# First norm with a weight spread by products, meta queries two blocks earlier, output projections in a held order

## The chip, the cores and the metric

The kernel runs on one core of a Trainium2 chip. A core has a matrix engine (TensorE, PE in the profile; its weight loads are a row of their own, PEld), VectorE (DVE), ScalarE (ACT), GpSimd (POOL) and SyncE (SP), which here issues every DMA. The metric is the device time of one execution, in microseconds; less is better. Where the time goes is read from one execution that the hardware profiler recorded.

## The reference

Two layers of a hybrid decoder, on 1024 tokens of 1024 columns with 16 learned meta tokens ahead of them (1040 rows), all in fp32:

```
h = rms_norm(x, norm_g)                       # row factor times weight
z = h @ w_in                                  # 1024 x 6408: aq ak av ag | mq mk mv mi mf mo mgate
ya = window_attention(rope(norm(q)), rope(norm(k)), v, sink) * silu(ag)   # 16 heads, 2 kv heads
hm = mlstm(silu(conv(mq, mk)), mv, mi, mf)    # 4 heads, chunkwise, with a carried state
ym = rms_norm(hm) * sigmoid(mo) * silu(mgate)
x  = x + concat(ya, ym) @ w_out               # 2048 x 1024
```

The window is 128 keys; the meta tokens are visible to every query and are themselves queries in the first layer. The meta rows are dropped at the end, so the second layer does not compute their attention or output (`first_q` is 1 there).

## The kernel before, in words

Rows are cut into nine tiles (`TT`): tile 0 has the 16 meta rows, tiles 1 to 8 have 128 rows each. For the gates and the loads of activations the same rows are cut into three chunks of columns (`CH`: 272, 384, 384). Every fp32 product is made of three products in the fast fp32r format: both operands are split into a high and a low part, and high x high, high x low and low x high are accumulated in PSUM (`mm3`, L178). For the short tile 0, the three parts are stacked as 48 rows (`HM`), so that two products do.

**Weights.** A weight piece is loaded by SP into one of two raw buffers, copied to its high part by ACT and subtracted to its low part by POOL or DVE (`wpair`, L147, for w_in; `wout`, L168, for w_out). Eight pairs of high and low parts stand in a ring (`RING`). In `wout` DVE takes each third piece and POOL the other two.

**A layer** goes through these stages: keys and values (`kv_tasks`, L452), the first queries, eight pairs of heads j = 0 to 7 with gate and query projections woven in, the mLSTM heads with their projections woven in, and the output projection (from L1091), which at the end of layer 0 also norms the rows for layer 1.

**First norm** (layer 0, `first_norm`, L312). For each row tile ACT squares and sums both halves (L318), POOL multiplies the halves by the norm weight `G` (L320), which a DMA has spread over 128 partitions (L456), and POOL raises the mean square to -1/2 (L279). DVE multiplies by that factor (L282), PE transposes (L288), ACT and DVE split the result into `H` (L291, L292). Tile 0 comes first, and two tiles are normed ahead of the one that is projected (`projN`, L200).

**Attention.** Block b of a pair of heads runs in four steps that lie two and three blocks apart: s1 the scores and the softmax (L618), s2 the transposes of the probabilities (L657), s3 and s4 the products with the values (L682, L695). s3 and s4 share one PSUM bank, `O`. The queries of the meta tokens for the next pair are transposed in s3 of block 5 into free columns of that bank (`q_meta_turn`, L688), and split into the query stack behind s4 (`q_put`, L559 to L564: two ACT copies, two DVE subtractions). The next pair's block 0 reads them in s1 (L628).

**Output projection.** The 16 column blocks of the mixer's result lie in DRAM (`spool`), the last two in SBUF. All are loaded and split (L1096 to L1109). Then come four groups: tiles 0 to 4 for the left and the right 512 columns, then tiles 5 to 8 likewise. In a group each weight piece is multiplied with each tile of the group (`product`, L1123 to L1135), and one PSUM bank per tile collects the sum; banks are dealt from three pools in turn. At the end of a group, for each tile: load the residual `xr` (L1154), add (L1157), store, and in layer 0 square for the next norm, in place in the bank (L1162). In the second half of columns, the norm of the tile follows (`norm_tile`, L274). In the last group the last eight pieces are held back, and each tile is finished alone.

**What sets the order.** The program is traced once; a planner then runs it in a simulated timeline and fixes the order of each engine's instructions by readiness and by the order in which they were traced. Semaphores enforce the dependencies; each engine then works its list strictly in order. `pin` (L68) makes PE's instructions keep the traced order among themselves while `in_order[0]` is set: in the first queries and the attention, but before the change not in the first norm, the mLSTM and the output projections. `tc.high_priority` lifts instructions in the planner's heap. Tile pools (16 units of 1152 columns, five of 384 (`t`), four of 512 (`p512`), two raw buffers) make an instruction wait until a buffer is free.

## Time and profile before

| | |
|---|---|
| median of 3 runs | 1997.38 us (1996.06 to 1997.59) |
| profiled execution | 1995.97 us, its span 1994.2 us |
| PE busy | 1916.2 us, 96% of the span |
| DVE, ACT, POOL busy | 55%, 53%, 47% |
| mean granted PE clock | 0.990 |
| DMA | 147.71 MB, mean 74 GB/s |

How to read it: a row of the timeline has start, duration, engine, line and operation, output and inputs, and in brackets how long the engine was idle before and what released it. A row of the waits has who waited for what, the total in microseconds, how often, and the longest. A row of a window has its stretch and length, then for PE, PEld, DVE, ACT and POOL the busy time with the number of instructions, then the granted PE clock, the DMA engines' share and GB/s. A row of a group has line, operation, shapes and count, then busy time and mean nanoseconds, then the idle time before. Matmuls are pipelined, so that a busy PE row need not be PE at its peak; idle time in it, though, is real.

### The profile page before, as it was taken

How to read it: one execution, taken by the hardware profiler on the slowest of the kernel's cores; microseconds unless marked ns; L12 is line 12 of the kernel's file. 1: busy time of each engine (PE TensorE's matmuls, PEld its weight loads, DVE VectorE, ACT ScalarE, POOL GpSimd, SP SyncE). 2: the span in 40 equal slices, each digit the busy share in tenths (PEclk: the TensorE clock that was granted, in tenths of full speed). 3: DMA queues.
4: the chain of work that ended last, by engine and by line, in shares of the span. 5: the costliest groups of instructions: out<-in, count | busy, mean ns of one | idle time of the engine just before them, and what ended most of it. 6: DMA issues, size and time to landing. Idle time of an engine off the chain costs nothing. (4 is left out here: it accounts for less than half of the span.)

```text
span 1994.2 us, 36168 instructions
## 1 busy us (share of the span) xinstructions
PE 1916.2 (96%) x12823; PEld 1806.1 (91%) x12823; DVE 1099.9 (55%) x2969; ACT 1062.6 (53%) x3133; POOL 929.9 (47%) x1116
## 2 busy tenths in 40 slices
PE   6999899999999999989999999999999999999899
PEld 6899899999999999867879999999999999997787
DVE  8767767666445364541435677776573636347111
ACT  5567767655454544642324678777364545446221
POOL 7544544335555454553335345444365453646331
PEclk9999999999999999999999999999999999999999
DMA  5111111111212122453541111112122221217443
GB/s 160 43 33 42 42 44 37 35 53 45 57 47 69 36 59 58 146 170 115 162 144 49 48 36 51 45 36 58 38 58 62 39 76 38 61 47 232 145 141 106
DMA packets 149796, 147.71 MB, mean 74 GB/s; under 512 B 14952, under 2 KB 122768, under 8 KB 149616
## 3 DMA queue, kind: packets, MB, share of 16 engines
q1 hardware_dynamic: 149616, 145.41, 25.1%
q8 instruction: 101, 1.65, 0.4%
q14 instruction: 79, 0.65, 0.1%
HBM read 122.01 MB, written 23.29 MB: 73 GB/s over the span
## 5 line engine op out<-in xcount | busy, mean ns | idle before, releaser
L183 PE MATMUL pj<-H,RING 128*128 128x384 f32 (+2 forms) x3456 | 578.4, 323 | 0.3 <-ACT t L838 0.3
L183 PEld LDWEIGHTS pj<-H,RING 128*128 128x128 f32 x3456 | 546.1, 189 | 2.9 <-issue 0.7
L160 POOL TENSOR_TENSOR RING<-raw,RING 128x512 fp32r<-128x512 f32 (+1 forms) x196 | 260.6, 1337 | 137.8 <-ACT RING L159 125.4
L222 PE MATMUL pj<-RING,H 128*128 128x256 f32 (+1 forms) x1920 | 270.0, 287 | 1.9 <-DVE w1k L190 1.9
L222 PEld LDWEIGHTS pj<-RING,H 128*128 128x128 f32 x1920 | 244.0, 190 | 2.3 <-DVE w1k L190 2.2
L222 PE MATMUL pj<-H,RING 128*128 128x384 f32 (+2 forms) x1152 | 217.7, 327 | 3.0 <-DVE u L564 3.0
L175 POOL TENSOR_TENSOR RING<-raw,RING 128x512 fp32r<-128x512 f32 x88 | 115.0, 1311 | 196.8 <-ACT RING L174 192.4
L183 PE MATMUL pj<-RING,H 128*128 128x256 f32 x1536 | 200.8, 285 | 2.6 <-DVE H L292 1.5
L183 PEld LDWEIGHTS pj<-RING,H 128*128 128x128 f32 x1536 | 189.0, 189 | 4.0 <-DVE H L292 1.7
L174 ACT ACTIVATE RING<-raw 128x512 fp32r<-128x512 f32 x128 | 80.7, 632 | 202.2 <-DMA raw<-in_w_out_dram 134.1
L222 PEld LDWEIGHTS pj<-H,RING 128*128 128x128 f32 x1152 | 180.7, 191 | 3.8 <-PE T L668 1.3
L159 ACT ACTIVATE RING<-raw 128x512 fp32r<-128x512 f32 (+1 forms) x196 | 122.9, 629 | 73.3 <-DMA raw<-in_w_in_dram 48.2
L713 POOL TENSOR_TENSOR u<-u,w1k 128x128 f32<-128x128 f32 (+1 forms) x136 | 63.4, 466 | 176.8 <-DVE w1k L709 169.4
L175 DVE TENSOR_TENSOR RING<-raw,RING 128x512 fp32r<-128x512 f32 x40 | 31.5, 788 | 194.0 <-ACT RING L174 194.0
L679 POOL TENSOR_SCALAR_AFFINE_SELECT p<-p 128x512 fp32r<-128x512 f32 x112 | 72.2, 645 | 133.7 <-DVE p L675 131.1
L649 ACT ACTIVATE t<-S,mx 128x145 f32<-128x145 f32 (+1 forms) x272 | 100.3, 373 | 62.6 <-DVE mx L646 54.5
L882 POOL TENSOR_TENSOR p<-u,p 128x258 fp32r<-128x258 f32 x64 | 46.7, 730 | 169.2 <-ACT p L881 169.1
L1135 PE MATMUL pj<-RING,H 128*128 128x512 f32 x352 | 112.9, 400 | 7.1 <-DVE p L1157 5.8
L1135 PE MATMUL pss<-RING,H 128*128 128x512 f32 x352 | 113.5, 402 | 1.3 <-ACT H L1104 1.3
L824 DVE SCALAR_TENSOR_TENSOR t<-u,cw,t 128x384 f32<-128x384 f32 (+1 forms) x144 | 109.1, 757 | 2.6
L628 PE MATMUL S<-u 128*128 128x272 f32 (+2 forms) x544 | 87.5, 280 | 19.3 <-DVE u L563 16.3
L654 ACT ACTIVATE t<-t,mx 128x144 f32<-128x144 f32 (+1 forms) x272 | 97.6, 406 | 13.6 <-DVE mx L651 13.1
(342 smaller groups left out, 3834.0 us busy)
## 6 DMA issues: line engine op xcount, KB each, us to landing
raw<-in_w_out_dram SPq DMA_DIRECT2D x128, 256.0 KB, 2.8
raw<-in_w_in_dram SPq DMA_DIRECT2D x100, 256.0 KB, 2.8
raw<-in_w_in_dram SPq DMA_DIRECT2D x192, 128.0 KB, 2.3
spool<-u SPq DMA_DIRECT2D x56, 192.0 KB, 1.9
p<-x SPq DMA_DIRECT2D x24, 256.0 KB, 4.4
t<-spool SPq DMA_DIRECT2D x28, 192.0 KB, 3.5
p<-spool SPq DMA_DIRECT2D x28, 192.0 KB, 3.6
u<-em SPq DMA_DIRECT2D x8, 576.0 KB, 6.9
```

Of the source, the lines that this page charges most:

```text
L159: sc.activation(hi, raw[:, :, 0:o], AF.Copy)
L160: eng.tensor_tensor(lo, raw[:, :, 0:o], hi, op=ALU.subtract)
L174: sc.activation(hi, raw, AF.Copy)
L175: (ve if i % 3 == 2 else gp).tensor_tensor(lo, raw, hi, op=ALU.subtract)
L183: pin(pe.matmul(out, a, b, start=(i == 0), stop=(i == n - 1)))
L222: pin(pe.matmul(out(), x, y, start=(k + i == 0), stop=(k == n - 1 and i == 2)))
L628: pin(pe.matmul(S[:p, h, o + 2 - 2 * h:o + 2 - 2 * h + kn], lq, Ks[i][:, k0:k0 + kn], start=(i == 0), stop=(i == 1)))
L649: sc.activation(P[:p, 145 * h:145 * h + 145], S[:p, h, 1 + 127 * h:146 + 127 * h], AF.Exp, bias=mx[:p, 0, h:h + 1], accum_out=mx[:p, 1, h: ...
L654: sc.activation(Pn, Pn, AF.Copy, scale=mx[:p, 2, h:h + 1])
L679: gp.affine_select(OW, HL, [[0, 4], [1, 128]], ALU.is_ge, 0.0, base=0, channel_multiplier=-1)
L824: ve.scalar_tensor_tensor(z, RAW[:, t0 + i:t0 + i + n], wcol(i), z, ALU.mult, ALU.add)
L1135: pin(pe.matmul(ps[:p, :], a, b, start=(i + n == 0), stop=(i == 15 and n == len(terms) - 1)))
```

## The change

**First norm.** The norm weight is loaded as one row, and two products with a row of ones spread it over 128 partitions into two PSUM banks. One DVE operation per half multiplies the rows by factor and weight at once, in place (`norm_pre`), instead of a POOL and a DVE operation; `norm_tile` is cut into `norm_pre` and `norm_half`. Tiles are taken in the order 1, 2, 0, 3 to 8; the loads of the first tile stand ahead of the constants, and the rope tables, masks and parameters come later. ACT's squares of a tile are placed behind the evacuation of an earlier tile (`tc.issue_after`), the rope tables behind the last power on POOL, and the conv parameters' transpose behind PE's last key and value product. The first queries' weights are asked for at the fourth tile.

**Meta queries.** The transpose for the next pair is placed in block 3 instead of block 5.

**Output projections.** Loading and splitting the activations is a function of column block and chunk (`y_split`): chunks 0 and 1 are interleaved with the weights of the first group, chunk 2 with those of the second. Banks rotate over six. Each group ends with a tail of three pieces (six in the last group), in which each tile is finished alone. The residual's load is placed behind the group's last weight load. Squares are written to another bank (`pt`). POOL splits all of a group's first nine pieces; from the tenth on DVE and POOL take turns. In layer 0 the norm of tiles 0 to 4 is taken from DRAM again and made in the third group, the one of tiles 5 to 8 in the last group, as half tiles between products (`turns`); three half tiles are carried into the keys and values of layer 1 (`carry`). From the second group on, PE keeps the traced order.

```diff
     cst = cp.tile([128, 166], F32, name="cst")
-    sy.dma_start(cst, I["cst"])
...
-        sy.dma_start(raw, I["w_out"][l][k * 128:(k + 1) * 128, c0:c0 + 512])
+        w_load[0] = sy.dma_start(raw, I["w_out"][l][k * 128:(k + 1) * 128, c0:c0 + 512]).ins
         hi, lo = [pair[:, a].rearrange("p a b -> p (a b)")[:, 0:512] for a in range(2)]
         sc.activation(hi, raw, AF.Copy)
-        (ve if i % 3 == 2 else gp).tensor_tensor(lo, raw, hi, op=ALU.subtract)
+        (ve if i > 8 and i % 2 else gp).tensor_tensor(lo, raw, hi, op=ALU.subtract)
...
-    def norm_tile(t, xh, ssq_ap, gbc):
...
+    def norm_pre(t, xq, ssq_ap, gbc):
...
-        gp.tensor_tensor(v[:p, 1:2], v[:p, 0:1], nhalf[:p, 0:1], op=ALU.pow)
-        for g in range(2):
-            if gbc is None:
-                ve.tensor_scalar(xh[g][:p, :], xh[g][:p, :], v[:p, 1:2], None, ALU.mult)
-            for i in range(2 if gbc is not None else 0):
-                xs = xh[g][:p, 256 * i:256 * i + 256]
-                ve.scalar_tensor_tensor(xs, xs, v[:p, 1:2], gbc[2 * g + i][:p, 0:256], ALU.mult, ALU.mult)
...
+        mark["POOL"] = gp.tensor_tensor(v[:p, 1:2], v[:p, 0:1], nhalf[:p, 0:1], op=ALU.pow).ins
+        for x, g in zip(xq, gbc):
+            ve.scalar_tensor_tensor(x[:p], x[:p], v[:p, 1:2], g[:p, 0:x.shape[1]], ALU.mult, ALU.mult)
+
+    def norm_half(t, g, xs):
+
+        t0, p = TT[t]
+        ps = bank("pt")
...
+            pin(pe.transpose(ps[:, k * p:(k + 1) * p], xs[k // n][:p, k % n * 128:k % n * 128 + 128], ident[:p, :p]))
+        src = ps[:, 0:4 * p].rearrange("p (k t) -> p k t", k=4)
+        hi = H[:, 4 * g:4 * g + 4, t0:t0 + p]
+        mark["ACT"] = sc.activation(hi, src, AF.Copy).ins
+        ve.tensor_tensor(H[:, 8 + 4 * g:12 + 4 * g, t0:t0 + p], src, hi, op=ALU.subtract)
...
     def first_norm(t, xt, G):
...
+        order = tc.issue_after(evac[-3]) if len(evac) > 2 else nullcontext()
...
-        xg = []
-        for i in range(2):
-            j = bank("pss") if i else bank("po")
-            sc.activation(j[:p, :], xt[:p, 512 * i:512 * i + 512], AF.Square, accum_out=st[:p, i:i + 1])
-            y = p512(F32)
-            gp.tensor_tensor(y[:p, :], xt[:p, 512 * i:512 * i + 512], G[:p, 512 * i:512 * i + 512], op=ALU.mult)
-            xg.append(y)
-        norm_tile(t, xg, st[:p, 0:2], None)
+        xh = [xt[:, 512 * i:512 * i + 512] for i in range(2)]
+        with order:
+            for i in range(2):
+                sc.activation(bank("po")[:p, :], xh[i][:p, :], AF.Square, accum_out=st[:p, i:i + 1])
+        norm_pre(t, xh, st[:p, 0:2], G)
+        norm_half(t, 0, xh[0:1])
+        evac.append(mark["ACT"])
+        norm_half(t, 1, xh[1:2])
...
         def kv_tasks():
+            ts = list(range(9))
+            kg = w1k()
+
+            def consts():
+                for i, (c, o) in enumerate(((0, 64), (0, 72), (1, 72), (1, 64))):
+                    gp.tensor_tensor(qrt[:, :, 8 * i:8 * i + 8], kcs[:, c], kg[:, o:o + 8]
+                                     .rearrange("p (a c) -> p a c", a=1).to_broadcast([128, 9, 8]), op=ALU.mult)
+                gp.tensor_scalar(qrt[:, :, 16:24], qrt[:, :, 16:24], -1.0, None, ALU.mult)
...
             if l == 0:
-                xt = {0: load_tile(0)}
-                G = unit()
-                sy.dma_start(G[:, 0:D], I["norm_g"][0].partition_broadcast(128))
-                xt[1], xt[2] = load_tile(1), load_tile(2)
-            if l == 0:
+                ts = [1, 2, 0, 3, 4, 5, 6, 7, 8]
+                gr = unit()
+                sy.dma_start(gr[0:1, 0:D], I["norm_g"][0:1, :])
+                xt = {1: load_tile(1)}
+                sy.dma_start(cst, I["cst"])
+                one = gr[0:1, D:D + 128]
+                ve.memset(one, 1.0)
+                G = [bank("pss") for _ in range(2)]
+                for i in range(2):
+                    pe.matmul(G[i], one, gr[0:1, 512 * i:512 * i + 512], start=True, stop=True)
                 ws = [unit() for _ in range(2)]
                 wg = wgroup(l, [(C_AK, 256)],
                             [ws[i // 2][:, 528 * (i % 2):528 * (i % 2) + 528].rearrange("p (a b) -> p a b", a=2)
...
+                for t in ts[1:4]:
+                    xt[t] = load_tile(t)
+                sy.dma_start(kcs.rearrange("p a b c -> p (a b c)"), I["kcs"])
+                load_kg()
+                for t in ts[4:]:
+                    xt[t] = load_tile(t)
+                sy.dma_start(mask, I["mask"])
+                rows = load_rows()
+                parameters()
+                for t in ts[:2]:
+                    first_norm(t, xt[t], G)
...
-            if l == 0:
-                rows = load_rows()
-                for t in range(3, 9):
-                    xt[t] = load_tile(t)
-                sy.dma_start(mask, I["mask"])
-                sy.dma_start(kcs.rearrange("p a b c -> p (a b c)"), I["kcs"])
-                parameters()
-                for t in range(2):
-                    first_norm(t, xt[t], G)
...
+                load_kg()
+                consts()
...
-            for t, (t0, p) in enumerate(TT):
-                if l == 0 and t + 2 < 9:
-                    first_norm(t + 2, xt[t + 2], G)
+            for i, t in enumerate(ts):
+                p = TT[t][1]
+                if l == 0 and i + 2 < 9:
+                    first_norm(ts[i + 2], xt[ts[i + 2]], G)
+                if l == 0 and i == 3:
+                    with tc.issue_after(mark["ACT"]):
+                        for _ in range(4):
+                            wq[0].more()
                 ps = projN(wg, t, 256)
+                if l > 0 and t != 1 and carry:
+                    carry.pop(0)()
                 ve.tensor_copy(KR[:p, t, :], ps[:p, 0:128])
                 sc.activation(VR[:p, t, :], ps[:p, 128:256], AF.Copy, scale=0.5)
                 if t == 0:
                     v_meta()
                 if t == 5:
                     k_chain(kg, 0, 5)
+            if l == 0:
+                with tc.issue_after(mark["POOL"]):
+                    consts()
             k_chain(kg, 5, 9)
             if l == 0:
-                parameters2(rows)
+                with tc.issue_after(mark["PE"]):
+                    parameters2(rows)
...
                 pm, HL, OW = live.pop(b)
                 O = bank("O")
-                if b == 5 and j < 7 and first_q == 0:
+                if b == 3 and j < 7 and first_q == 0:
                     st["QM"] = O[:, 256:272]
                     q_meta_turn(j + 1, st["QM"])
...
-        for i, k in enumerate(order):
-            ylo[k] = unit(F32R)
-            for c, (t0, n, _) in enumerate(CH):
-                a = s0 if c == 0 else t0
-                if k < 14:
-                    y = p512(F32, t0 + n - a) if (i + c) % 2 else t384(t0 + n - a)
-                    sy.dma_start(y, spool[k, :, a:t0 + n])
-                else:
-                    y = ym[k - 14][:, a:t0 + n]
...
+
+        def y_split(i, c):
+
+            k = order[i]
+            t0, n, _ = CH[c]
+            a = s0 if c == 0 else t0
+            if k not in ylo:
+                ylo[k] = unit(F32R)
...
+            hi = H[:, k, a:t0 + n]
+            sc.activation(hi, y, AF.Copy)
+            if a == 0:
...
-        pools = ["pj", "pss", "po"]
-        nb = 0
-        for grp in (range(first_q, 5), range(5, 9)):
...
+        pools = ["pj", "pj", "pss", "pss", "po", "po"]
+        nb = [0]
+        turns = []
+
+        def product(ps, i, t, w):
...
+        def result(ps, t, hf):
+
+            t0, p = TT[t]
+            c0 = 512 * hf
+            xr = p512(F32)
...
+            with tc.issue_after(w_load[0]):
+                sy.dma_start(xr[:p, :], src)
...
+            ve.tensor_tensor(xr[:p, :], ps[:p, :], xr[:p, :], op=ALU.add)
...
+            if hf == 1 and t > 4:
+                x0 = [t384(256) for _ in range(2)]
+                for i, x in enumerate(x0):
+                    sy.dma_start(x[:p, :], x1[t0:t0 + p, 256 * i:256 * i + 256])
+            sy.dma_start(x1[t0:t0 + p, c0:c0 + 512], xr[:p, :])
+            sc.activation(bank("pt")[:p, :], xr[:p, :], AF.Square, accum_out=ssq[:p, t, hf:hf + 1])
+            if hf == 1 and t > 4:
+                norm_later(t, x0 + [xr[:, 0:256], xr[:, 256:512]])
+
+        def norm_later(t, xq):
+            norm_pre(t, xq, ssq[:TT[t][1], t, :], gbc)
+            turns.extend(lambda g=g: norm_half(t, g, xq[2 * g:2 * g + 2]) for g in range(2))
+
+        def norm_again(t):
+
+            t0, p = TT[t]
+            x = [p512(F32) for _ in range(2)]
+            for i in range(2):
+                sy.dma_start(x[i][:p, :], x1[t0:t0 + p, 512 * i:512 * i + 512])
+            norm_later(t, [y[:, o:o + 256] for y in x for o in (0, 256)])
+
+        def turn(least=1):
+            if len(turns) >= least:
+                turns.pop(0)()
+
+        for g, (grp, hf) in enumerate([(grp, hf) for grp in (range(first_q, 5), range(5, 9)) for hf in range(2)]):
+            c0 = 512 * hf
+            in_order[0] = g > 0
+            pss_t = {}
+            for t in grp:
+                pss_t[t] = bank(pools[nb[0] % 6])
...
+            cut = 10 if g == 3 else 13
+            chunks = ((0, 1), (2,), (), ())[g]
+            for i in range(cut):
+                for c in chunks:
+                    y_split(i, c)
+                w = wout(l, order[i], c0, i)
                 for t in grp:
-                    pss_t[t] = bank(pools[nb % 3])
-                    nb += 1
...
-                cut = 16 - 8 if hf == 1 and grp[-1] == 8 else 16
-                for i, k in enumerate(order[:cut]):
-                    w = wout(l, k, c0, i)
-                    for t in grp:
-                        product(i, k, t, w)
-                tail = [(i, order[i], wout(l, order[i], c0, i)) for i in range(cut, 16)]
-                for t in grp:
-                    for i, k, w in tail:
-                        product(i, k, t, w)
...
-                    sc.activation(pss_t[t][:p, :], xr[:p, :], AF.Square, accum_out=ssq[:p, t, hf:hf + 1])
-                    if hf == 1:
-                        x0 = p512(F32)
-                        sy.dma_start(x0[:p, :], x1[t0:t0 + p, 0:512])
-                        norm_tile(t, [x0, xr], ssq[:p, t, :], gbc)
+                    product(pss_t[t], i, t, w)
+                if g == 2 and not last:
+                    if i > 2:
+                        turn()
+                    if i % 2 and i < 10:
+                        norm_again(i // 2)
+            for i in range(cut, 16):
+                for c in chunks:
+                    y_split(i, c)
+            tail = [(i, wout(l, order[i], c0, i)) for i in range(cut, 16)]
+            for t in grp:
+                for i, w in tail:
+                    product(pss_t[t], i, t, w)
+                    if g == 3 and i == 12:
+                        turn(3)
+                if g == 3:
+                    turn(2)
+                result(pss_t[t], t, hf)
+        in_order[0] = False
+        carry[:] = turns
```

116 lines of the change are left out of this document (53 added, 63 removed).

## The prediction

> **What bounds the kernel now.** I read the head of the page, then PE's waits by stage, then the timeline at each wait, last the granted clock behind the longest ones. Each engine runs its instructions in the order in which they were placed, so what counts is what stands ahead of what.
>
> ```profile
> span 1994.2 us, 36168 instructions
> PE 1916.2 (96%) x12823; PEld 1806.1 (91%) x12823; DVE 1099.9 (55%) x2969; ACT 1062.6 (53%) x3133; POOL 929.9 (47%) x1116
> ```
>
> PE is the bound: what takes a hole out of PE's row is worth that hole, and hardly anything else is worth something. The holes lie in three places, one for each part of the change. The first is the start (timeline of PE, POOL and ACT):
>
> ```profile
> 7.00 5.28 POOL L320 TENSOR_TENSOR p<-u 16x512 f32<-16x512 f32 x4 [1.34 <-DMA u<-in_norm_g_dram]
> 8.15 0.60 ACT L318 ACTIVATE po<-u 128x512 f32<-128x512 f32 x1 [3.47 <-DMA u<-in_x_dram]
> 15.91 3.52 PE L206 MATMUL pj<-RING,HM 128*48 128x256 f32 x15 [1.22 <-DVE RING L160]
> 20.66 0.51 PE L183 MATMUL pj<-RING,H 128*128 128x256 f32 x2 [0.25 <-ACT H L291]
> ...
> 31.70 1.69 PE L183 MATMUL pj<-RING,H 128*128 128x256 f32 x12
> 33.58 1.68 PE L183 MATMUL pj<-RING,H 128*128 128x256 f32 x12
> ...
> 52.59 2.03 PE L206 MATMUL pj<-RING,HM 128*48 128x256 f32 x16
> ...
> 62.89 3.01 PE L222 MATMUL pj<-RING,H 128*128 128x256 f32 x24
> ```
>
> The first whole tile is multiplied only at 20.66, and PE is dense for good from 62.89. The second place is the change from one pair of heads to the next in layer 0's attention; the third is the two output projections, of which the window counts the products begun in one stretch:
>
> ```profile
> PE S L628 <- DVE u L563: 15.4, 7, 5.9
> PE T L665 <- DVE ptm L676: 2.8, 1, 2.8
> ```
> ```profile
> 867.17 0.44 PE L1135 MATMUL pj<-RING,u 128*48 128x512 f32 x1 [2.25 <-POOL RING L175]
> ...
> 1047.07 1.97 PE L288 MATMUL pt<-cst,p 128*128 128x128 f32 x8 [2.00 <-DVE H L292]
> ...
> 1857.56 1.22 PE L1135 MATMUL pj<-RING,H 128*128 128x512 f32 x2 [5.85 <-DVE p L1157]
> ```
> ```profile
> 885.48:896.68 11.20, 7.86 (x21) 0.70 0.42 142
> ```
>
> Behind a hole the granted clock falls (the third number from the end; 1.00 is full):
>
> ```profile
> 244.00:252.00 8.00, 3.65 (x20) 3.51 (x21) 3.59 (x13) 4.51 (x16) 7.46 (x8) 0.57 0.32 91
> 329.00:334.00 5.00, 4.18 (x23) 4.04 (x24) 2.75 (x8) 1.93 (x9) 4.73 (x4) 0.66 0.30 83
> 1046.00:1051.00 5.00, 3.93 (x21) 3.93 (x22) 4.10 (x8) 2.60 (x6) 2.13 (x3) 0.66 0.24 64
> 1855.00:1863.00 8.00, 5.44 (x13) 4.37 (x14) 3.08 (x5) 2.31 (x4) 2.55 (x2) 0.57 0.65 212
> ```
>
> 0.66 over 5 us is 1.7 us of PE time lost; 0.57 over 8 us is 3.4 us, of which a part lies under the hole itself. I count 1.7 us each at 244, 329 and 1046, and 2.6 us at 1855, where products restart at 1857.56. The Trainium skill ("TensorE: Matmul & The Clock Gate", What's actually happening) asks for an idle window of about 3.4 us before the half rate. Here holes of 2.00 us (before 1047.07) did it, so the measurement decides; by the page the half rates at 329 and 1046 would have another cause and stay, 3.4 us less gain.
>
> **Part A, the start.** Removed: the spread of the norm weight by DMA (512 KB), 18 multiplications on POOL, 18 scalings on DVE. Added: two products of one row by 512 columns, 18 joint scalings (row, factor, weight from PSUM) on DVE. A whole tile comes first; tables and parameters come later.
>
> ```profile
> L282 DVE TENSOR_SCALAR p<-p,nv 128x512 f32<-128x512 f32 (+1 forms) x18 | 16.4, 922 | 4.1 <-POOL p L320 3.5 <-POOL nv L279 0.5
> ```
> ```profile
> L320 POOL TENSOR_TENSOR p<-u 128x512 f32<-128x512 f32 (+1 forms) x18 | 24.2, 1357 | 5.8 <-DVE nv L278 3.8 <-DMA u<-in_norm_g_dram 1.3 <-PE pt L288 0.7
> ...
> L279 POOL TENSOR_TENSOR nv<-nv,cst 128x1 f32<-128x1 f32 (+1 forms) x9 | 5.8, 644 | 5.1 <-DVE nv L278 5.1
> ```
> ```profile
> 4.00:8.00 4.00, 0.00 (x0) 0.00 (x0) 0.28 (x2) 0.68 (x3) 1.54 (x2) 1.00 1.00 321
> 8.00:52.00 44.00, 33.84 (x261) 31.75 (x261) 40.68 (x78) 26.84 (x69) 36.98 (x36) 1.00 0.45 143
> ```
> ```profile
> L601 DVE SCALAR_TENSOR_TENSOR u<-t,pj x48: 399/553/556, 92.2 to 1350.2; 128x384 f32<-128x384 f32 x32, 128x272 f32<-128x272 f32 x8, 128x256 f32<-128x256 f32 x8
> L755 PE MATMUL po<-cst,rw x4: 168/178/189, 442.0 to 1419.7; 1*36 1x1 f32 x4
> ```
> ```profile
> 1985.02 5.57 PE pj L1135 x24
> ...
> 1990.62 0.69 DVE p L1157
> ```
>
> DVE (40.68 us of 44) and POOL (36.98) are nearly full at the start. No row has the new scaling at 512 columns; L601, the same operation with one operand in PSUM, takes 0.399 us at 256 and 0.553 at 384, 1.2 ns a column, so about 0.70 at 512. Against 0.922 that takes 18 x 0.22 = 4 us from DVE, and POOL loses the 24.2 us of L320. The Trainium skill ("SBUF — State Buffer", SBUF: two separate sides) says that DVE and POOL exclude each other on one port pair while DVE runs a two-port mode or reads two SBUF inputs. L601's narrow spread (median 0.553, longest 0.556) agrees that an operand in PSUM escapes this; were the new scaling lengthened by half after all, 18 x 0.35 = 6 us would come back.
>
> The one-row product: the nearest row, L755, takes 0.178 us for one column; full products of 512 columns run at 5.57/24 = 0.23 us. Two of them, each in one to four passes, at full to half clock, are 0.4 to 3.7 us. They run on an idle PE while the tile lands and is squared, so they cost nothing; without that cover, some 2 us.
>
> When does tile 1 start? Its rows landed at 8.15 behind the spread weight; at 321 GB/s, 512 KB are 1.6 us, so it lands at about 6.5 (sooner by its place in the queue). Two squares and their sums some 1.4 us (2 x 0.60 and a little), small DVE operations 0.3 (my estimate), the power 0.64, scaling 0.70, four transposes 0.4 (the half-tile period 33.58 - 31.70 = 1.88, less 12 products at 3.01/24), evacuation 0.6 like a square: 4.0. First product at 10.5 instead of 20.66. From 20.66 to 62.89, PE did sixteen half tiles at 1.88, 2.0 of L206 and 24 products of L222 (3.0 at full clock): 35 us of work in 42.2. With the short tile moved behind (2.0 at full clock, not 3.5) the same point comes at 10.5 + 35 + 2 = 47.5: a ceiling of 15 us. The other end is DVE's: if it sets the end, the gain is the 4 us of the scalings, or nothing if the late tables hold up the queries. I take **10 us**, nearer the ceiling because the waits of DVE and POOL on each other go too; bounds 0 and 15.
>
> **Part B, meta queries at block 3.** Nothing is added: a transpose, two ACT copies and two DVE subtractions, of 16 columns, move up two of nine blocks.
>
> ```profile
> 123.42 0.49 PE L628 MATMUL S<-u 128*16 128x16 f32 x4 [0.93 <-DVE u L563]
> ...
> 241.16 0.45 PE L704 MATMUL O<-p,u 128*128 128x256 f32 x2
> ...
> 248.27 0.50 PE L628 MATMUL S<-u 128*16 128x16 f32 x4 [5.90 <-DVE u L563]
> ```
> ```profile
> 244.94 0.71 ACT L654 ACTIVATE t<-t,mx 128x144 f32<-128x144 f32 x2
> ```
>
> The next pair's first score needs meta queries whose split ends 7.1 us after the last product in their bank (241.16 to 248.27) in the worst case. Three pairs lie between 123.42 and 248.27, so a block is 125/27 = 4.6 us and two are 9 us: all seven waits are covered. Ceiling 15.4 + 1.7 + 1.7 = 18.8 us. What is late next: the transposes of the pair's last block need L654, which ended at 245.65, so some 2 us of the long hole stay; and the O products of block 4 now wait for the split in their one bank as those of block 6 did. I leave 1 us a pair for both: **12 us**, bounds 4 (only the short waits' half) and 18.8.
>
> **Part C, output projections.** The loads of activations are interleaved with the weights, their last third goes to the second group; banks rotate over six; a tail of three weights spreads the results; squares no longer write the bank; POOL, not DVE, splits the first nine weights of a group; from the second group on PE's order is held.
>
> ```profile
> 890.79 0.69 DVE L175 TENSOR_TENSOR RING<-raw,RING 128x512 fp32r<-128x512 f32 x1 [7.45 <-ACT RING L174]
> 891.52 0.68 DVE L1156 TENSOR_TENSOR p<-pj,p 16x512 f32<-16x512 f32 x1
> ...
> 1856.21 0.69 DVE L175 TENSOR_TENSOR RING<-raw,RING 128x512 fp32r<-128x512 f32 x1 [8.16 <-ACT RING L174]
> 1856.82 0.68 DVE L1157 TENSOR_TENSOR p<-pj,p 128x512 f32<-128x512 f32 x1
> ```
>
> This is the cause of both large holes: the additions that free the banks stand on DVE behind a split whose weight had not landed. With POOL on the first nine weights nothing of the kind stands ahead. In layer 0, some 20 products (4.6 us) took the 11.2 us from 885.48: 6.6 lost. Layer 1 lost 5.85 + 2.6 = 8.4. With 2.25 before 867.17 and 2.0 + 1.7 at 1047 the ceiling is 21 us. I take 5.5 + 7.5 + 1 + 2.5 = 16.5, and pay 3 us for the held order, where a late transpose stops PE: in the last group a tail of 18 products (4.2 us) has to cover an addition (0.69), a square (0.60 and its sum), the power and two scalings, about 3.5 us. **13.5 us**, bounds 0 and 21. The very end, product, addition and store, stays.
>
> **Sum.** 10 + 12 + 13.5 = 35.5. The profiled execution took 1995.97 us, 1.8 more than its span; the median of the runs, 1997.38, is 1.4 above it. 1995.97 - 35.5 + 1.4 = **1962 us**.
>
> **The rivals.** (1) DVE sets the start, A gives 2: 1970. For it: 40.68 of 44. Against: part of those durations is POOL's doing.
> (2) The attention's holes only move, B gives 4: 1970. For it: L676 already stands second among the waits. Against: L676 held PE once in the stage, so the other six changes of pair have their transposes ready.
> (3) Norm turns and evacuations stop the held PE, C gives 3: 1972. For it: 4.2 us against 3.5. Against: only 1047 shows such a chain late.
> (4) Slower: in the held order PE follows the supply of weights.
>
> ```profile
> raw<-in_w_out_dram SPq DMA_DIRECT2D x128, 256.0 KB, 2.8
> L174 ACT ACTIVATE RING<-raw 128x512 fp32r<-128x512 f32 x128 | 80.7, 632 | 202.2 <-DMA raw<-in_w_out_dram 134.1
> L175 POOL TENSOR_TENSOR RING<-raw,RING 128x512 fp32r<-128x512 f32 x88 | 115.0, 1311 | 196.8 <-ACT RING L174 192.4
> ```
>
> Two raw buffers give a weight every (2.8 + 0.63 + 1.31)/2 = 2.4 us; PE uses one in 14 x 0.23 = 3.2 us or, with four tiles, 2.8. If the loads of activations, now in the first two groups, push landing to 6.5 us, a weight takes 4.2: (1.0 + 1.4) x 32 = 77 us lost in the two layers, and with A and B 1995.97 - 22 + 77 + 1.4 = 2052. It outweighs A and B (22 us) from a landing of about 4.7. Against it: the median of 2.8, with the same loads packed closer in the first group.
> (5) The planner puts the moved work where it was, so the change doesn't do what it says: 1996.
> (6) Everything near its ceiling: 1945.
>
> **Chances.** Forecast 0.52 (1950 to 1969), (1), (2), (3) 0.11 each, (4) 0.06, (5) 0.04, (6) 0.05. The range 1946 to 1983 leaves out (4), (5) and the edges of joint failures of (1) to (3). A measurement of this kernel tells about 0.2%, 4 us, from no change: faster 0.90, same 0.04, slower 0.06.
>
> **What would show it.** A: first product of a 128-row tile before 12 us, PE dense from 50, scalings of 0.70. B: no score waits for L563's 16-column form. C: at either group change no PE wait over 1 us and no half clock. I am wrong if PE waits for RING in the second groups, if DVE is still behind at 50 us, or if PE waits for the norm's transposes.

## The result and the profile after

The kernel after takes 1963.07 us (median of four runs, 1961.97 to 1963.54); the kernel before took 1997.49 us beside it (1996.06 to 1998.13). The ratio is 0.9828, with a 95% interval of 0.9811 to 0.9845: 34 us less, where 1962 us had been forecast. The profiled execution took 1962.62 us, its span is 1960.9 us. The head of its page has:

```profile
PE 1912.5 (98%) x12827; PEld 1801.3 (92%) x12827; DVE 1095.6 (56%) x2962; ACT 1062.0 (54%) x3133; POOL 915.8 (47%) x1106
```

PE's busy time hardly moved (1916.2 to 1912.5 us): what went is idle time between its products. To see where, I cut both executions at the same instructions of each layer: the first score, the first transpose of the gates (L737, now L772), the first product of the output projection (L1135, now L1169), and at the very last product. These are rows of PE's timeline taken by source line; each has the shortest, median and longest duration and, behind it, the first and last start in the stretch looked at. Before:

```profile
L628 PE MATMUL S<-u x9: 171/232/391, 85.7 to 89.8; 128*16 128x16 f32 x4, 128*128 128x144 f32 x4, 128*128 128x272 f32 x1
L737 PE MATMUL po<-cst,GT x1: 271/271/271, 432.2 to 432.2; 128*36 128x128 f32 x1
L1135 PE MATMUL pss<-RING,H x6: 391/394/505, 830.1 to 833.0; 128*128 128x512 f32 x6
L628 PE MATMUL S<-u x8: 228/282/289, 1094.6 to 1096.5; 128*128 128x144 f32 x4, 128*128 128x272 f32 x4
L737 PE MATMUL po<-cst,GT x1: 273/273/273, 1410.2 to 1410.2; 128*36 128x128 f32 x1
L1135 PE MATMUL pj<-RING,H x6: 388/417/789, 1801.3 to 1805.4; 128*128 128x512 f32 x6
L1135 PE MATMUL pj<-RING,u x8: 392/394/398, 1985.3 to 1990.2; 128*128 128x512 f32 x8
```

After:

```profile
L663 PE MATMUL S<-u x12: 170/272/397, 77.1 to 81.7; 128*16 128x16 f32 x4, 128*128 128x144 f32 x4, 128*128 128x272 f32 x4
L772 PE MATMUL po<-cst,GT x1: 271/271/271, 419.1 to 419.1; 128*36 128x128 f32 x1
L1169 PE MATMUL pss<-RING,H x8: 388/396/499, 815.1 to 819.7; 128*128 128x512 f32 x8
L663 PE MATMUL S<-u x8: 228/282/289, 1070.6 to 1072.5; 128*128 128x144 f32 x4, 128*128 128x272 f32 x4
L772 PE MATMUL po<-cst,GT x1: 270/270/270, 1387.5 to 1387.5; 128*36 128x128 f32 x1
L1169 PE MATMUL pj<-RING,H x8: 388/394/496, 1776.1 to 1779.6; 128*128 128x512 f32 x8
L1169 PE MATMUL pss<-RING,u x11: 391/393/398, 1949.8 to 1956.7; 128*128 128x512 f32 x11
```

The differences of neighbouring starts, in us:

| stage | before | after | gain | part (forecast) |
|---|---|---|---|---|
| start, to the first score | 85.7 | 77.1 | 8.6 | A (10) |
| layer 0, attention | 346.5 | 342.0 | 4.5 | B (12) |
| layer 0, mLSTM | 397.9 | 396.0 | 1.9 | |
| layer 0, output projection, to layer 1's first score | 264.5 | 255.5 | 9.0 | C (13.5 in all) |
| layer 1, attention | 315.6 | 316.9 | -1.3 | unchanged code |
| layer 1, mLSTM | 391.1 | 388.6 | 2.5 | |
| layer 1, output projection | 188.9 | 180.6 | 8.3 | C |

So the sum came out as forecast, but not its terms: B brought less than half, C about a quarter more. Layer 1's attention tells how far such a row can be trusted: in that stage nothing was edited in any kernel below, and over their fourteen traces it takes 314.6 to 319.5 us. Two single traces of a stage can thus lie almost 5 us apart for no reason of the edit, and a smaller difference is read as an effect only where several traces agree on it.

**The start** shows what was to be seen there. The timeline of PE, then the scaling's row by groups, after:

```profile
2.44 3.75 PE L485 MATMUL pss<-u 1*128 1x512 f32 x4 [2.44 <-DMA u<-in_norm_g_dram]
10.40 5.99 PE L184 MATMUL pj<-RING,H 128*128 128x256 f32 x24 [0.41 <-ACT H L296]
...
L285 DVE SCALAR_TENSOR_TENSOR u<-u,nv,pss 128x512 f32<-128x512 f32 (+1 forms) x18 | 12.5, 739 | 0.2 <-POOL nv L283 0.2
```

The first whole tile is multiplied at 10.40 us (20.66 before; 10.5 forecast), and a scaling takes 0.74 us (0.70 forecast). The one-row products, four records for two products, are at the upper end of their bounds (3.75 us) and lie on a PE that has nothing else.

**Layer 0's attention.** PE's waits from 77 to 419 us, after:

```profile
PE O L727 <- DVE w1k L744: 4.5, 5, 1.7
PE T L700 <- DVE ptm L711: 4.0, 2, 3.1
PE O L727 <- DVE u L599: 2.6, 4, 1.1
PE pj L224 <- DVE u L636: 2.3, 2, 1.3
PE pj L224 <- DVE u L599: 1.9, 2, 1.0
PE S L663 <- ACT t L684: 1.0, 1, 1.0
```

The 15.4 us of score waits for the 16-column split (L563, now L598) are gone, and waits that were not in the list before, or were under 1 us, have come: O products behind L744 and L599, others behind L599 and L636. With two smaller rows the list sums to 17.7 us, that of before to 20.6, so the waits became only 2.9 us shorter in all. About as much came from the clock: this stage has three stretches of lower granted clock before and two after, and by the windows in the prediction and in the account of it below they cost 6.8 us of PE time before and 3.4 after. (A part of such a stretch lies under a hole, so the two savings add up to more than the 4.5 us of the table.)

**Output projections.** All of PE's waits from 1770 us to the end, after:

```profile
PE po L904 <- DVE w1k L968: 1.1, 1, 1.1
PE po L1169 <- POOL RING L176: 0.3, 1, 0.3
PE po L1169 <- DVE RING L176: 0.2, 1, 0.2
PE pj L1169 <- ACT H L1143: 0.2, 1, 0.2
```

The hole of 5.85 us is closed (L904 is the last mLSTM product), and the longest wait at any change of group is 0.3 us.

### The profile page after: what moved, and what is told of

It reads as the page before. It is cut to its first block, busy times and chain, and to the rows that moved or that the text cites. A ratio compares the mean times of both kernels' runs of the same rounds, so it can differ in the third digit from the quotient of the medians.

```text
span 1960.9 us, 36174 instructions
## 1 busy us (share of the span) xinstructions
PE 1912.5 (98%) x12827; PEld 1801.3 (92%) x12827; DVE 1095.6 (56%) x2962; ACT 1062.0 (54%) x3133; POOL 915.8 (47%) x1106
## 5 line engine op out<-in xcount | busy, mean ns | idle before, releaser
L176 POOL TENSOR_TENSOR RING<-raw,RING 128x512 fp32r<-128x512 f32 x96 | 125.8, 1316 | 178.9 <-ACT RING L175 162.9
L1169 PE MATMUL pss<-RING,H 128*128 128x512 f32 x384 | 120.5, 395 | 0.0
L1169 PE MATMUL pj<-RING,H 128*128 128x512 f32 x352 | 109.8, 394 | 0.2 <-ACT H L1143 0.2
L744 DVE TENSOR_TENSOR w1k<-O,w1k 64x128 f32<-64x128 f32 (+1 forms) x272 | 74.6, 274 | 37.8 <-ACT w1k L742 35.2
L877 DVE SCALAR_TENSOR_TENSOR t<-t,pj 128x384 f32<-128x384 f32 (+2 forms) x48 | 24.5, 510 | 125.7 <-ACT t L876 125.5
```

Source lines behind the costliest of these rows:

```text
L176: (ve if i > 8 and i % 2 else gp).tensor_tensor(lo, raw, hi, op=ALU.subtract)
L744: ve.tensor_tensor(y[64 * h:64 * h + 64, :p], O[0:64, p * h:p * h + p], up[0:64, p * h:p * h + p], op=ALU.add)
L1169: pin(pe.matmul(ps[:p, :], a, b, start=(i + n == 0), stop=(i == 15 and n == len(terms) - 1)))
```

## The experiments

All times are medians; the ratio is to the kernel before, run beside each. "Attention" is layer 0's, "projection 0" and "projection 1" are the stages of the table above, measured in the same way.

| kernel | us | ratio (95%) | first score | attention | projection 0 | projection 1 |
|---|---|---|---|---|---|---|
| before | 1997.49 | 1 | 85.7 | 346.5 | 264.5 | 188.9 |
| after | 1963.07 | 0.9828 (0.9811 to 0.9845) | 77.1 | 342.0 | 255.5 | 180.6 |
| e1: after, queries at block 5 | 1969.38 | 0.9864 (0.9844 to 0.9884) | 76.4 | 348.0 | 258.7 | 180.3 |
| e2: before, queries at block 3 | 1988.39 | 0.9964 (0.9952 to 0.9976) | 83.5 | 341.2 | 262.7 | 188.9 |
| e3: after, order not held | 1966.71 | 0.9854 (0.9837 to 0.9871) | 76.7 | 342.1 | 261.9 | 179.9 |
| e4: after, old split rule | 1963.56 | 0.9841 (0.9825 to 0.9858) | 78.1 | 340.5 | 255.4 | 180.8 |
| e5: before, new split rule | 1994.56 | 0.9987 (0.9977 to 0.9998) | 85.9 | 347.0 | 266.4 | 185.0 |
| e9: after, no tail | 1957.52 | 0.9801 (0.9786 to 0.9815) | 76.9 | 341.8 | 254.8 | 178.9 |
| e10: after, no tail, old rule | 1971.50 | 0.9871 (0.9856 to 0.9886) | 77.2 | 341.5 | 256.8 | 188.3 |
| e11: before, with the tail | 1993.95 | 0.9983 (0.9974 to 0.9992) | 86.1 | 349.2 | 260.3 | 188.0 |
| e6: after, short tile first | 1966.72 | 0.9855 (0.9838 to 0.9871) | 85.0 | 340.1 | 254.7 | 180.5 |
| e7: after, weight spread by DMA | 1960.60 | 0.9823 (0.9807 to 0.9839) | 76.8 | 341.4 | 254.8 | 179.2 |
| e13: e7, scaled in two operations | 1970.02 | 0.9874 (0.9858 to 0.9891) | 85.6 | 339.9 | 254.8 | 180.5 |
| e12: e9, queries in a score bank | 1956.49 | 0.9801 (0.9787 to 0.9816) | 76.5 | 339.5 | 254.7 | 178.9 |

### Part B: what the meta queries are worth

e1 takes the kernel after and turns the queries at block 5:

```diff
-                if b == 3 and j < 7 and first_q == 0:
+                if b == 5 and j < 7 and first_q == 0:
```

> The kernel after, with the meta queries turned at block 5 again instead of block 3, nothing else. Landmarks of the two traces put the gain between the first scores and the end of layer 0's attention at 4.4 us (8.6 us ahead at the first score, 13.1 us at the first product of the gates), where the prediction had 12 us. Theory M (the holes only moved: the split of block 3 now holds up the next product in the one bank O): 1967 to 1968 us, i.e. 4 to 5 us slower than after, and the score waits for the 16-column subtraction come back, 10 to 16 us of them, while the waits of L727 for L744 and L599 shrink from 8.6 us to under 3. Theory P (the prediction's step, 12 us, part of it hidden by other changes): 1973 to 1977 us.

e2 does the opposite edit on the kernel before.

> The kernel before, with the meta queries turned at block 3, nothing else: part B by itself. Theory M: 1992 to 1994 us (4 to 5 us faster), the score waits of 15.4 us gone and waits of the same kind at the O bank in their place, 5 to 10 us. Theory P: 1983 to 1987 us (12 us faster).

PE's waits in layer 0's attention: the first of e1, then two of e2:

```profile
PE S L663 <- DVE u L598: 15.2, 7, 5.9
```
```profile
PE O L692 <- DVE w1k L709: 4.6, 5, 1.7
...
PE O L692 <- DVE u L564: 2.6, 4, 1.1
```

The waits come and go with that one number, and the new ones are the same in e2 as in the kernel after, so they belong to this part and not to its neighbours. In e1 all waits of the stage sum to 20.6 us again, and windows of 0.66, 0.57 and 0.66 over 5, 12 and 5 us (from 154, 236 and 407 us) make 8.6 us lost to the clock, against 3.4 in the kernel after. In this pair, then, more of the gain comes from the clock than from the waits: one long hole became several short ones, behind which the clock was low for a shorter time. The size is best read over all traces of the table: with block 5 (before, e1, e5, e11) the stage takes 346.5 to 349.2 us, median 347.5; with block 3 (the other nine without e12) 339.9 to 342.1, median 341.4. The two sets don't touch; the difference is 6.1 us. The times agree: e2 is 7.6 us under the kernel before beside it (4.8 to 9.6 us by the interval). That is more than theory M's 4 to 5 and about half of theory P's 12.

e12 asks whether bank O is what took the rest. It starts from e9 (the kernel after without the tail, part C) and puts the transposed queries into unused columns of a score tile:

```diff
-                    st["QM"] = O[:, 256:272]
+                    st["QM"] = SS[blk[0] % 2][:, 1, 448:464]
```

> The kernel after, with no tail in the first three groups of the output projections (as in the run that took 1957.52 us) and with the transposed meta queries put into free columns of a score tile instead of the one bank O. Theory M (part B's gain was given back at bank O: waits of L727 for L744 and for the 16-column subtraction, 8.6 us in the kernel after, of which the subtraction's 2.6 us and part of L744's are due to the change): 2 to 6 us less in layer 0's attention, 339 us from first score to first gates instead of 342, and 1952 to 1956 us. Rival (the waits at O come from L744's own chain of copies and additions, which stays): 341 to 343 us for the attention, 1956 to 1959 us, the waits of L727 as before.

Rows of PE's waits in its attention:

```profile
PE pj L224 <- DVE u L636: 3.3, 3, 1.1
PE O L727 <- DVE w1k L744: 2.7, 4, 1.7
PE pj L224 <- DVE u L599: 2.6, 2, 1.3
PE S L663 <- DVE u L599: 1.5, 3, 0.5
```

The O products no longer wait for L599, and for L744 only 2.7 us instead of 4.5. But scores now wait for L599 (1.5), and products of the other stream wait more for L599 and L636. The stage takes 339.5 us, 0.4 under the shortest of the others: not told apart from no gain. That PE's wait follows the short chain on ACT and DVE, whichever bank the queries lie in, fits these rows; no run takes that chain itself away.

### Part C: what closed the holes of the output projections

e4 gives every third weight's low half back to DVE in the kernel after:

```diff
-        (ve if i > 8 and i % 2 else gp).tensor_tensor(lo, raw, hi, op=ALU.subtract)
+        (ve if i % 3 == 2 else gp).tensor_tensor(lo, raw, hi, op=ALU.subtract)
```

> The kernel after, with the low half of every third weight of the output projections split on DVE as before (instead of on POOL for the first nine of a group), nothing else. Theory S1 (a split that waits for its weight ahead of the additions on DVE was the cause of both large holes, as the prediction has it): holes of 2 to 6 us return at the group changes, 1970 to 1980 us. Theory S2 (six banks in turn make the additions' delay harmless, since the next group's banks are free already): 1962 to 1966 us, and PE shows no wait over 1 us there though DVE's additions stand behind the split.

Nothing changed, though DVE's timeline has what was held to be the cause:

```profile
1821.22 0.69 DVE L176 TENSOR_TENSOR RING<-raw,RING 128x512 fp32r<-128x512 f32 x1 [9.86 <-ACT RING L175]
1821.83 1.28 DVE L1186 TENSOR_TENSOR p<-pj,p 128x512 f32<-128x512 f32 x2
```

DVE stood for 9.86 us at the split of a weight, two additions were queued behind it, and PE did not wait for them: its only wait for an addition in layer 1's projection is one of 0.4 us, 48 us later. So I took the tail away, first alone (e9), then with the old rule (e10):

```diff
-            cut = 10 if g == 3 else 13
+            cut = 10 if g == 3 else 16
```

> The kernel after, with no tail in the first three groups of the output projections: all 16 weights go over all tiles and the results come together at the end of the group, as before. The rule on POOL and DVE stays. Theory T: the additions are again all due at the change of group, holes of 1 to 4 us come back at several of the six changes, 1967 to 1976 us. Theory S1: the splits do not stand ahead of the additions, so nothing is lost, 1961 to 1965 us.

> The kernel after, with no tail in the first three groups and with every third weight split on DVE as before: both undone together. The rule alone, undone, changed nothing (1963.56 against 1963.07 us). Theory R (tail and rule are two covers of one hole, and either is enough): 1970 to 1980 us here, with waits of PE for the addition back, while each alone stays at 1961 to 1966. Theory T: about the same as without the tail alone, 1967 to 1976 us. Theory N (neither: the hole went with the moved loads of the activations and the held order): 1961 to 1966 us.

With both undone the hole of layer 1 is back in its old size. The longest of PE's waits in layer 1's projection of e10, and DVE's timeline there:

```profile
PE pj L1169 <- DVE p L1186: 5.9, 1, 5.9
...
1830.91 0.69 DVE L176 TENSOR_TENSOR RING<-raw,RING 128x512 fp32r<-128x512 f32 x1 [5.58 <-ACT RING L175]
1831.52 1.28 DVE L1186 TENSOR_TENSOR p<-pj,p 128x512 f32<-128x512 f32 x2
```

Theory R holds in layer 1: rule and tail are two covers of the same hole. Projection 1 takes 188.3 us with neither, 178.9 with the rule alone, 180.8 with the tail alone, 180.6 with both. The tail adds nothing to the rule: e9's stage is the shortest of these, and its span is 1958.5 against 1960.9 us. By the ratios its gain over the kernel after is about 5 us, but the two intervals overlap (0.9815, 0.9811), so a gain is not shown.

In layer 0 neither matters much (256.8 with both undone, against 254.8 to 255.5). The counterparts on the kernel before show what else was late there. e5 has the new rule alone, e11 the tail alone:

```diff
-        (ve if i % 3 == 2 else gp).tensor_tensor(lo, raw, hi, op=ALU.subtract)
+        (ve if i > 8 and i % 2 else gp).tensor_tensor(lo, raw, hi, op=ALU.subtract)
```

> The kernel before, with one rule of the change: POOL instead of DVE splits the first nine weights of each group of the output projections. Theory S1 (the prediction's step: the additions stand on DVE behind a split whose weight has not landed, and POOL takes those splits away): both holes close, 13 us by the prediction's terms (5.5 + 7.5), so 1982 to 1985 us. Theory T (what closes them in the kernel after is the tail of three weights, which gives the results one by one while the group still multiplies, so that the additions are no longer all due at the change of group): the rule by itself helps only where the late split is its own, 1988 to 1996 us, and a hole of over 2 us is left at one change of group at least.

```diff
-                cut = 16 - 8 if hf == 1 and grp[-1] == 8 else 16
+                cut = 16 - 8 if hf == 1 and grp[-1] == 8 else 13
```

> The kernel before, with a tail of three weights in the first three groups of the output projections (the last keeps its eight), nothing else. Theory T: the two large holes close though every third split stays on DVE, 1982 to 1988 us. Theory S1: DVE is still behind the late split when the banks are wanted, 1992 to 1998 us.

PE's longest wait in layer 0's projection of e5, and below it the longest row of e11's waits in the last stretch, from 1920 us on:

```profile
859.05 0.63 PE L1135 MATMUL pj<-RING,u 128*48 128x512 f32 x1 [5.20 <-ACT RING L174]
```
```profile
PE pj L1135 <- ACT RING L174: 2.5, 3, 1.4
```

Each edit alone brings 2 to 2.5 us of time, of the 17 us by which the two stages became shorter: the hole at the addition goes, and PE stops for weights instead. So one cover is enough in the kernel after, where the weights keep coming, and brings little in the kernel before. In e5 PE stands 5.20 us for the high half of a weight, and not at the change of group, where the additions start at 889.92 us, but within the first group. SP issued that weight's load only at 853.66 us (in the kernel before the first such load of this stretch went out at 849.51), right behind loads of activations (L1100), for which it had waited 2.8 us in the 9 us before, and ACT, which had stood 2.6 us for activations since 853 us, copied the weight at 858.27 us as soon as it had landed. In e11 PE waits for weights in the last group. What in the change keeps the weights coming in layer 0 was not undone by itself. By elimination, which is an argument and not a run, it is what is left of the change: activations loaded and split between the weights and a third of them a group later, residuals loaded behind the weights, squares off the banks. The place of e5's late load in SP's queue points to the first of these.

e3 lets the planner order PE's products in the output projections:

```diff
-            in_order[0] = g > 0
+            in_order[0] = False
```

> The kernel after, without the held order of PE's products in the output projections (the planner orders them, as before), nothing else. Theory S (the gain of part C comes from the splits leaving DVE's queue, six banks in turn, and the split loads; the held order itself neither costs nor brings anything): 1962 to 1966 us. Theory H (the held order is what closes the group changes): 1968 to 1982 us, with PE waits of over 1 us back at a group change. The prediction had priced the held order at a cost of 3 us: by it the time would be 1960.

The largest of PE's waits from the end of layer 0's projection to layer 1's first score:

```profile
PE pj L184 <- ACT u L520: 4.3, 1, 4.3
```

Both group changes stay clean, but layer 1's keys and values now stop for 4.3 us (0.5 us in the kernel after), and projection 0 takes 261.9 us instead of 254.7 to 258.7. By this one trace the held order brings 3 to 7 us in this stage; in the time it is 4 to 5, with intervals of the two ratios that overlap by a little, so the gain is likely and not shown. In layer 1 it shows no cost (179.9 without, 180.6 with it).

### Part A: what made the start earlier

e6 puts the short tile first again, e7 spreads the weight by a DMA into SBUF:

```diff
-                ts = [1, 2, 0, 3, 4, 5, 6, 7, 8]
+                ts = list(range(9))
...
-                xt = {1: load_tile(1)}
+                xt = {0: load_tile(0)}
```

> The kernel after, with the short tile of 16 rows first again (order 0, 1, 2, ... for the loads, the norm and the products), nothing else. By the prediction's account of part A the short tile costs 3.5 us ahead of the rest at half clock and 2.0 us behind it, and tile 1 is landed and scaled one tile later: the first 128-row product comes 1 to 3 us later than its 10.4 us, the first score 1.5 to 4 us later than its 77.1 us, 1964 to 1967 us in all. Rival (DVE and POOL set the end of the start stage, so the order of the tiles is no matter): first score at 76 to 78 us, 1962 to 1964.

```diff
-                sy.dma_start(gr[0:1, 0:D], I["norm_g"][0:1, :])
                 xt = {1: load_tile(1)}
+                sy.dma_start(gr[:, 0:D], I["norm_g"][0].partition_broadcast(128))
...
-                for i in range(2):
-                    pe.matmul(G[i], one, gr[0:1, 512 * i:512 * i + 512], start=True, stop=True)
+                G = [gr[:, 512 * i:512 * i + 512] for i in range(2)]
```

> The kernel after, with the norm weight spread to 128 partitions by a DMA into SBUF behind the rows of tile 1, instead of by two one-row products into PSUM; the joint scaling of rows, factor and weight then reads both large operands from SBUF. By the prediction's account: 512 KB at 321 GB/s delay the first scaling by 1 to 2 us, and a scaling that stays at 0.70 us changes nothing more: first 128-row product at 11.5 to 13 us, 1964 to 1966 us. Rival D (two operands in SBUF hold DVE and POOL against each other, as the shared port would have it): the 18 scalings take 1.0 us and more, and the start loses 4 to 8 us: 1967 to 1971. Rival N (the spread is hidden and the operand's place is no matter): 1962 to 1964.

e7 shows the first score at 76.8 us, and its scaling is no slower:

```profile
L285 DVE SCALAR_TENSOR_TENSOR u<-u,nv 128x512 f32<-128x512 f32 (+1 forms) x18 | 12.7, 742 | 1.2 <-POOL nv L283 1.1
```

It takes 0.742 us with both operands in SBUF, 0.739 with one in PSUM. The test is weak, though, because POOL, without its 18 products, hardly ever ran beside a scaling. The norm at the end of layer 0 is a better one: there the same line scales 256 columns at a time with the weight in SBUF, while POOL splits weights. Rows of L285 in the kernel after, with shortest, median and longest duration in ns:

```profile
L285 DVE SCALAR_TENSOR_TENSOR u<-u,nv,pss x18: 729/740/750, 7.2 to 35.3; 128x512 f32<-128x512 f32 x16, 16x512 f32<-16x512 f32 x2
L285 DVE SCALAR_TENSOR_TENSOR p<-p,nv,w1k x28: 464/480/1590, 922.0 to 1026.8; 128x256 f32<-128x256 f32 x24, 16x256 f32<-16x256 f32 x4
```

With the weight in SBUF nine of the 36 (eight more write `t`) took 1.4 to 1.6 us: all nine met a split of POOL, and each ended 0.27 or 0.28 us after it. The Trainium skill ("SBUF — State Buffer", SBUF: two separate sides) has DVE and POOL exclude each other where DVE reads two SBUF inputs. These nine agree with it.

In e7 only the last two scalings met more of POOL than a power. They kept their 0.73 us, but two operations of POOL beside them (L467) took 1.05 and 0.89 us. In the kernel after, where the last two scalings read the weight from PSUM, L467 kept its 0.34 us, and the scalings their 0.74. So e7 loses nothing on DVE because POOL was mostly idle, and the place of the weight would matter where it isn't. For the time here, the two products are worth no more than a DMA behind the first tile's rows.

e13 keeps e7's spread and goes back to two operations, POOL's product and DVE's scaling:

```diff
+            gp.tensor_tensor(y[i][:p, :], xh[i][:p, :], G[i][:p, :], op=ALU.mult)
...
-            ve.scalar_tensor_tensor(x[:p], x[:p], v[:p, 1:2], g[:p, 0:x.shape[1]], ALU.mult, ALU.mult)
+            ve.tensor_scalar(x[:p], x[:p], v[:p, 1:2], None, ALU.mult)
```

> The kernel after with the weight spread by DMA (the run that took 1960.6 us and showed the first score at 76.8 us), and besides with rows and weight multiplied on POOL and the product scaled on DVE, 18 times each, as before, instead of in one operation; the order of tiles and loads stays the change's. By the prediction's account of part A: 18 x 0.22 = 4 us come back to DVE, and POOL gets its 24 us back, in a start where DVE is busy for 31.7 of the 40 us from 12 to 52: 1964 to 1968 us, first score at 80 to 84 us. Rival (the earlier start came from the order of tiles and loads alone; DVE and POOL have the room): 1960 to 1963 us, first score at 76 to 78 us.

Its groups up to the first score, and its window from 12 to 52 us; below it the same window of e7 (PE, PEld, DVE, ACT, POOL):

```profile
L331 POOL TENSOR_TENSOR p<-u 128x512 f32<-128x512 f32 (+1 forms) x18 | 24.8, 1394 | 8.6 <-DMA u<-in_norm_g_dram 5.8 <-DMA u<-in_x_dram 1.9 <-PE pt L295 0.8
L285 DVE TENSOR_SCALAR p<-p,nv 128x512 f32<-128x512 f32 (+1 forms) x18 | 12.0, 691 | 2.5 <-POOL nv L283 2.5
...
12.00:52.00 40.00, 35.34 (x267) 32.73 (x266) 33.23 (x74) 24.18 (x65) 35.53 (x34) 1.00 0.32 109
```
```profile
12.00:52.00 40.00, 37.08 (x293) 35.47 (x292) 31.71 (x84) 25.82 (x69) 17.27 (x21) 1.00 0.38 124
```

The first score is at 85.6 us, as before the change: 8.8 us of part A hang on the joint scaling. The 18 scalings of DVE cost about the same either way (12.0 us here, 12.7 in e7, and DVE is busy for 33.23 and 31.71 us of the window); POOL has 24.8 us more and is busy for 35.53 us of 40 instead of 17.27. On POOL each tile's power stands behind such products: the first starts at 8.77 us, and PE's first transposes at 11.09, against 8.38 in e7; the second tile's scaling waits 2.5 us for its power.

The mean of 0.691 us hides two kinds of scaling:

```profile
L285 DVE TENSOR_SCALAR p<-p,nv x18: 468/478/1494, 10.6 to 46.4; 128x512 f32<-128x512 f32 x16, 16x512 f32<-16x512 f32 x2
```

Undisturbed it takes 0.47 us. One that begins while POOL runs a product or a split of two operands ends 0.28 or 0.29 us after that operation, whatever its own length. Eleven of the 18 were held up in this way before (mean 0.922 us; at 42.30 us, for example, one took 1.22 us beside L320), seven in e13. The two means differ by how often and how long the two engines met, and not by the scaling.

e6 lost nearly as much at the start, its first score at 85.0 us, by another way: PE waits 5.8 us for ACT, whose timeline says why. SP's timeline follows:

```profile
30.21 0.69 ACT L458 ACTIVATE VM<-w1k,cst 64x128 fp32r<-64x128 f32 x2 [7.89 <-DMA w1k<-u]
```
```profile
13.28 0.50 SPq L340 DMA_DIRECT2D w1k<-in_mlstm_conv_w_dram  x1
...
26.44 2.49 SPq L454 DMA_DIRECT2D w1k<-u  x4
```

With the short tile first, ACT is due at its values from 22.3 us on, but they come by a transfer (L454), and on SP that transfer stands behind 13 small loads of parameters, 13.28 to 24.6 us, and one of a weight. ACT waits 7.89 us for it, with the squares and copies of the next tiles behind. Behind the hole the granted clock is 0.57 in the 8 us from 29 us on. In the kernel after the transfer comes at 28.5 us and ACT waits 0.5 us for it. e6's time is only 3 to 5 us above that of the kernel after; in the cuts of the traces the other 5 us went in the two attention stages (1.9 and 2.1 us shorter in e6) and projection 0 (0.8), all of them differences within what such stages scatter. So part A needs both: the order of the tiles undone loses 7.9 us of its first score, the joint scaling 8.8.

## Why the prediction was right, and where not

**Part A (10; measured 8.6, and 8.8 by e13).** The first product came within 0.1 us of its forecast, but that is luck, as two errors of the chain of tile 1 cancelled. ACT's timeline after:

```profile
4.57 0.60 ACT L326 ACTIVATE po<-u 128x512 f32<-128x512 f32 x1 [2.49 <-DMA u<-in_x_dram]
...
9.23 0.63 ACT L158 ACTIVATE RING<-u 128x512 fp32r<-128x512 f32 x1 [0.25 <-DMA u<-in_w_in_dram]
9.77 0.58 ACT L296 ACTIVATE H<-pt 128x512 fp32r<-128x512 f32 x1
```

The rows had landed at 4.57 us, not at 6.5. From there to the product it took 5.8 us, not 4.0: the first four transposes took 1.1 us (8.03 to 9.14; 0.4 in the sum), the evacuation then stood behind the copy of a weight on ACT, and a weight's split on DVE stood ahead of the scaling; neither is in the sum. The cost of the one-row products was hidden as said. Wrong in its mechanism is the step "against 0.922 that takes 18 x 0.22 = 4 us from DVE": the row did fall from 16.4 to 12.5 us, but the 0.922 was in good part time in which a scaling was held up by POOL (0.47 us without it), the joint scaling is longer than that (0.74), and by e13 the price of the two operations is POOL's load, which the prediction put second. What stood against rival 1 there, that part of DVE's durations is POOL's doing, was right.

**Part B (12; measured 6.1).** The step that failed is "I leave 1 us a pair for both". All seven waits were covered, but bank O, T and the other stream gave back more than that: 6.1 of a ceiling of 18.8 remained. One row of before had pointed to T: L676, second in the list. Rival 2 (the holes move, B gives 4) described the mechanism, the forecast was between. The half clock fell about as priced (1.7 us in each of two places). Before, it cost 3.4, 1.7 and 1.7 us of PE time in this stage (the windows at 244 and 329 of the prediction, and the one quoted here first); after, 1.7 us twice, in the 5 us from 238 (the second fence) and from 402 us:

```profile
415.00:420.00 5.00, 4.71 (x20) 4.74 (x21) 3.49 (x9) 2.24 (x4) 1.98 (x4) 0.66 0.21 52
```

```profile
238.00:243.00 5.00, 4.63 (x24) 4.66 (x25) 2.74 (x8) 3.48 (x13) 4.84 (x5) 0.66 0.34 101
```

**Part C (13.5; measured 17.3, and some of the 4.4 us at the ends of the mLSTM stages).** Layer 1's 7.5 was right in cause and nearly in size (8.3), only that the rule had a second cover in the tail. Layer 0's 5.5 had only half of its cause: the additions did start late, behind a split (890.79 in the prediction's lines), but PE, which went on in the one bank that was free, stood for the ring of weights (waits of 0.57, 1.81 and 0.69 us between 888 and 894 us), and with the rule alone a wait for weights of 5.20 us opens elsewhere in the group (e5). The step "pay 3 us for the held order" had no cost behind it; by e3 the held order more likely brings 4 to 5 us, since the planner's own order held up layer 1's keys and values. "Banks rotate over six", counted as part of the change, was no change: three pools of two, taken in turn, were six before as well. The first product's wait for its activations was not in the sum. It is the one part of the mLSTM rows that can be named; layer 1 before, and 0.2 us in the list of after:

```profile
PE pj L1135 <- ACT H L1104: 1.3, 1, 1.3
```

Rivals 3 (the held PE stops), 4 (weights late) and 5 (the planner undoes it) did not come; what rival 4 feared was seen where the loads are not interleaved, in e5.

**The sum** was right by luck: B's miss (7.5 us between the two traces, 6 over all of them) was made good by C's 4 and the mLSTM stages' 4.4, while A fell 1.4 short and layer 1's attention gave 1.3 back within its scatter. The 4.4 is in part scatter as well: between the medians over the four traces of kernels built on the one before and the ten built on the one after, the two mLSTM stages differ by 0.6 and 2.1 us. Nothing in the working foresaw that balance. Its signs came: a first product before 12 us, no score wait for the 16-column split, and no wait over 1 us and no lower clock at a change of group. What the prediction had right is where the holes were and that PE's idle time sets the gain; its three terms were off by 14% to 49%.

e12, with no tail and the queries in a score bank, is the fastest of all: 1956.49 us, a span of 1953.0 against 1960.9. Its ratio's interval, up to 0.9816, still touches that of the kernel after.

## What to carry to other kernels

A wait that is moved is worth what the chain behind it leaves: here 15.4 us of waits, moved, brought 6.1 us, and much of that because shorter holes cost less of the granted clock. So look in the list of waits for the row that is second now, and at the clock behind the longest hole. Before a hole is put down to one cause, undo the suspected cause in the mended kernel and apply it alone to the old one: here one hole had two covers, either enough in the mended kernel and neither worth much in the old one. Look at the single durations behind a mean before you price an operation by it: 0.922 us was a mix of 0.47 and of up to 1.5. And one small transfer behind a dozen parameter loads stopped an engine for 8 us here: the order on the load queue is part of the order of the tiles.

## What had not been expected of the hardware

A joint scaling of rows, factor and weight takes the same time with the weight in SBUF (0.742 us) as in PSUM (0.739). The scaling by the factor alone takes 0.47 us, but when it began while POOL ran a product or a split it ended some 0.28 us after POOL's operation and lasted up to 1.5 us; its mean (0.922 us before, 0.691 in e13) is a matter of how often the two met. The same held for the joint scaling of 256 columns with the weight in SBUF (0.47 us alone, up to 1.59 beside a split), and not for the two scalings with the weight in PSUM that met POOL (0.74 us).
